# Residual adds of mixer and FFN by accumulating transfers, one rule for the fast rstd, and a planner that knows a shared port

## The chip, the cores and the metric

The kernel runs on one core of one Trainium2 chip. The metric is the time of one execution on the device in microseconds (us), the median of several. The engines of the core run side by side, each in the order of its own queue: TensorE (PE, matmul), VectorE (DVE), ScalarE (ACT), GpSimd (POOL) and SyncE (SP, which here only issues transfers). They wait for each other and for the transfers (DMA) on semaphores.

## The reference

One layer of a streaming encoder, for 1024 prompt frames and 64 further frames of a running stream that share the weights: a token mixer, a SwiGLU FFN and a gated embedding, each added to the residual behind an RMSNorm.

```python
hn = _rmsnorm(h, pre_mix_g)
proj = hn @ w_in
...
mix = jnp.concatenate([y.astype(h.dtype), pool_out.astype(h.dtype)], axis=-1) @ w_out
h = h + _rmsnorm(mix, post_mix_g)
hn = _rmsnorm(h, pre_ffn_g)
f = (jax.nn.silu(hn @ w_gate) * (hn @ w_up)) @ w_down
h = h + _rmsnorm(f, post_ffn_g)
gate = jax.nn.sigmoid((h @ w_ple_gate).astype(f32))
e = (p_i @ w_ple_proj).astype(f32) * gate
h = h + _rmsnorm(e, ple_norm_g).astype(h.dtype)
```

The width is 1024, the FFN's 2816. What is left out above is the mixer's inside: a causal convolution, a chunked state-space scan with a SiLU gate, and pooling over trailing windows. The two lines of `h = h + _rmsnorm(...)` behind mixer and FFN are what the change touches.

## The kernel before

**Tiling.** Features lie on the 128 partitions, in eight pages (1024 features); tokens lie along the free dimension, 1088 of them in four chunks of 272 (0 to 3). Every fp32 operand of a matmul is split into a high and a low part, and a product takes three passes (high x high, low x high, high x low), each a matmul of 128x128 by 128x272. Most of ACT's casts (the high part) and DVE's subtractions `sub` (L400, the low part) make such pairs.

**Stages.** In-projection and convolution, scan and pooling, out-projection; behind it the mixer's end by chunk; then the FFN in two phases, in a Strassen-like form that works on pairs of chunks (`h_T`, `h_B` and their combinations are its inputs); behind it the FFN's end by chunk, and the gated embedding with `w_pg` (PE L493, L476).

**The mixer's end, `post_mix`.** Of a chunk, the squares of the out-projection are summed, and `rstd_job` makes 1/rms of it: PE sums over the partitions with four small matmuls (L511), DVE does nine operations on 68x4 (L516 to L545), and PE spreads the result over the partitions with four transposes (L549). Then `two(i)`, for each of four pairs of pages: x is loaded to a half page `xr` by SP; DVE multiplies the pages of `mixf` by rstd (L1402); POOL adds x (L1408, the letter 'G' in `XM`). When two pairs are added, SP stores them as h1 to DRAM. ACT squares the sum (L601), DVE adds the squares (L608, L619), a second `rstd_job` makes the rstd of h (tile `t_h`), and `norm` (L1433) multiplies by it. From this come `h_T` and `h_B`: cast (L1453), low part (L400), differences (L1465).

**The FFN's end, `post_ffn`.** The same with `f`: scale on ACT (L2057), load of h1 to `hr`, multiply (L2064), add on POOL (L2067, 'G' in `XF`) or on DVE (L2070, 'D'), cast to the high page of h (L2074), low page (L400). PE takes these pages at L493, in their order.

**The start.** `w_in0` comes in two halves, with the four x pages of the first chunk between and behind them, all by SP; ACT casts the weights (L827) and makes x (L731), and PE begins at L914.

**What sets the order.** The kernel's text isn't the order of the queues. The class `Layout` is a planner that runs when the kernel is built: every job is a generator that yields (engine, cost in us, wait), and the planner keeps one clock for each engine and puts the instruction that could start first next. PE's work is the base on which time goes forward (`tick`, cost of a matmul from `mmt`). On the chip, each engine then runs its queue in order, and waits where the estimate was too early. In `rstd_job`, the flag `f` (0 if `fast`, else 1) sets how long the sums and the transposes are held back in the plan after what they need: with `fast` not at all, without it the transposes by 3 pieces of PE's work.

Of the kernel before, what the change touches and what calls it, by code (L numbers as in the profile page):

```python
# [11 lines left out]
ALU = mybir.AluOpType  # L12
# [11 lines left out]
ORD_X = (0, 1, 2, 3)  # L24
# [10 lines left out]
XM, XF, XP = 'GGGG', 'GDGD', 'GDDD'  # L35
# [14 lines left out]
P_XP = 3  # L50
# [7 lines left out]
P_DTC = 4  # L58

# [4 lines left out]
TW = -1  # L64
X_LATE = 18
NK = 8
# [147 lines left out]
class Layout:  # L214
# [7 lines left out]
    def __init__(self):  # L222
        self.now = T0
        self.seq = 0
        self.jobs = []
        self.busy = {"A": BA, "D": BD, "G": 0.0}
        self.done = 0.0
        self.mem = 0.0
        self.rate = RATE
        self.fill = []  # L230
        self.filling = False
# [8 lines left out]
    def step(self, job):  # L240
        self.done = job["t"]
        try:
            req = next(job["gen"])
        except StopIteration:
            return False
        finally:
            self.done = 0.0
        job["req"] = req
        if not callable(req):
            wait = req[2] if len(req) > 2 else 0  # L250
            job["ready"] = max(job["t"] + (HOP if req[0] != job["eng"] else HOPS), wait) if isinstance(wait, At) else job["t"] + (0.04 if wait == TW else wait * self.PIECE if wait >= 3 else HOP if req[0] != job["eng"] else HOPS)
        return True
# [6 lines left out]
    def tick(self, length=None):  # L259
        self.now += (length or self.PIECE / 2)  # L260
        far = self.now + AHEAD
        while True:
# [35 lines left out]
            eng, cost = job["req"][:2]  # L298
            self.busy[eng] = job["t"] = start + cost
# [25 lines left out]
def trunk(ctx, tc, xT, par, wmix, wdt, poolw, wout, wff, wdn, wpg, wpp, pT, ssm0,  # L325
# [58 lines left out]

    cp = const.tile([P, PWIDTH], F32, name="cp")
# [28 lines left out]
    def wjob(name, src, tag, bufs, ready=None, width=2 * NK * P, raw=None, at=None, free=None, start=None, keep=lambda: 0):  # L414
# [3 lines left out]
        def gen():  # L418
# [29 lines left out]
            yield ("D", 1.23)  # L448
# [16 lines left out]
    def mmt(n):  # L465

        return (1.0625 * n + 14) / 2400
# [119 lines left out]
    class SumSq:  # L587
# [8 lines left out]
        def job(self, src, used):  # L596
# [7 lines left out]
            if first:  # L604
                self.acc = sq
            else:
                yield ("D", 0.8)
                ve.tensor_tensor(self.acc, self.acc, sq, ALU.add)  # L608
                n2.give(sq)
# [7 lines left out]
        def whole(self):  # L617
            yield ("D", 0.45)
# [109 lines left out]
    def x_split(c, k, rv, at, used):  # L728
# [3 lines left out]
        yield ("D", 0.51)  # L732
# [5 lines left out]
    def x_square(c, k, rv, at, used):  # L738
# [15 lines left out]
        if k:  # L754
            yield (add_e, 0.45 if add_e == "D" else 0.92)
# [75 lines left out]
    def w0_low(h, hs):  # L831
        yield ("D", 0.6)
# [15 lines left out]
    def x_job():  # L848
        for c in ORD_X[1:]:
            for k2 in range(4):  # L850
# [34 lines left out]
    def conv_post(i):  # L885
# [4 lines left out]
        for w_ in range(1, 4):  # L890
            yield ("D", 1.38)
# [36 lines left out]
    for i in range(4):  # L928
        donew(f"in{i}")
# [125 lines left out]
    def ssd(c):  # L1055
# [32 lines left out]
        yield ("D", 0.7, 0)  # L1088
# [6 lines left out]
        for b in range(4):  # L1095
            yield ("A", 0.24, 0)
# [14 lines left out]
        for g in range(2):  # L1111
            yield ("D", 0.68, 0)
# [6 lines left out]
        else:  # L1119
# [5 lines left out]
            yield ("D", 0.68, 0)  # L1125
# [58 lines left out]
    def pool_post(gi):  # L1184
# [7 lines left out]
        for step in range(gi + 1):  # L1192
# [4 lines left out]
            yield ("D", 1.25, 0)  # L1197
# [7 lines left out]
        yield ("D", 1.25)  # L1205
# [8 lines left out]
        yield ("D", 1.25, 1)  # L1214
        sub(ve, plo[:, HIST:], cur[:, HIST:], ph[:, HIST:])
        exts.give(cur)
        for c, (t0, L) in enumerate(CH):
# [9 lines left out]
            for s, ln, grp, pos in chunk_parts(c):  # L1227
                o = HIST + SEQ - f if grp else t0 - f
                yield ("A", 0.14 + ln * 0.0011, 1)
# [43 lines left out]
    def z_job(i, c, ps, zz):  # L1273
# [10 lines left out]
        for s, n, v in parts_view(i, c):  # L1284
            yield ("D", 0.12 + n * 0.00125, 1)
# [4 lines left out]
    def gate(c, zz):  # L1290
# [3 lines left out]
        for g in range(2):  # L1294
# [7 lines left out]
            yield ("D", 0.45)  # L1302
# [15 lines left out]
    def mix_split(c, i):  # L1318
# [3 lines left out]
        for s, n, v in parts_view(i, c):  # L1322
            yield ("D", 0.12 + n * 0.00125)
# [62 lines left out]
    def post_mix(c, mf, ss):  # L1386
# [7 lines left out]
        def two(i):  # L1394
            yield n2.ok
            xr = n2.take(f"xr{c}_{i}")
            yield ("S", 0, 0)
            at = dma(xr, xT[c][:, 2 * i:2 * i + 2], 2 * L)
# [7 lines left out]
            if XM[i] == "G":  # L1406
                yield ("G", 1.6, at)
                gp.tensor_tensor(v, v, xr, ALU.add)  # L1408
            else:
                yield ("D", 0.73, at)  # L1410
                ve.tensor_tensor(v, v, xr, ALU.add)
            n2.give(xr)
# [17 lines left out]
        def norm(m, r2, left):  # L1430
            v = mf[m // 4][:, m % 4, :]
            yield ("D", 0.45, 0)
# [8 lines left out]
    def hforms(p):  # L1441
# [5 lines left out]
        def form(f, src):  # L1447
# [4 lines left out]
            yield ("A", 0.78, 1)  # L1452
            ac.copy(vs[0], src)  # L1453

            def low():
                yield ("D", 1.06)
# [6 lines left out]
        def add(dst, x, y):  # L1463
            yield ("D", 1.06)
# [66 lines left out]
    def weight_stream(units):  # L1531
        def form(u, f, src):
# [22 lines left out]
            def low():  # L1555
                yield ("D", 0.15 + 0.133 * u.ks)
# [11 lines left out]
        def add(u, dst, x, y, op):  # L1568
            yield ("D", 0.15 + 0.133 * u.ks, 1)
# [60 lines left out]
    def evac(q, m):  # L1630
# [4 lines left out]
        def finish(blk, t):  # L1635
# [7 lines left out]
            else:  # L1643
                yield lambda: blk in q.gate.a
                g = q.gate.a[blk]
                yield ("D", tD)
# [56 lines left out]
    def aforms(q):  # L1703
# [5 lines left out]
        def form(f, t):  # L1709
# [7 lines left out]
            def low():  # L1717
                yield ("D", tD)
# [14 lines left out]
        def add(dst, x, y):  # L1733
            yield ("D", tD)
# [39 lines left out]
    def p_piece(c):  # L1774
# [7 lines left out]
        yield ("D", 0.73)  # L1782
# [7 lines left out]
    def proj_group(c, m):  # L1790
        def emit():
# [5 lines left out]
            def job():  # L1797
                yield nts.ok
                e_ = nt(f"e{c}_{m}")
                yield ("A", 0.48, 1)  # L1800
# [245 lines left out]
    def post_ffn(c, ss, prio):  # L2046
# [6 lines left out]
        def two(i):  # L2053
# [4 lines left out]
            yield n2.ok  # L2058
            hr = n2.take(f"hr{c}_{i}")
            yield ("S", 0, 0)  # L2060
            at = dma(hr, h1_d[c][:, 2 * i:2 * i + 2], 2 * L)
            yield lambda: bool(flag)
            yield ("D", 1.0, 0)
            ve.tensor_tensor(v, v, flag[0][:, :L].unsqueeze(1).broadcast_to([P, 2, L]), ALU.mult)  # L2064
            if XF[i] == "G":
                yield ("G", 1.6, at)
                gp.tensor_tensor(v, v, hr, ALU.add)  # L2067
            else:
                yield ("D", 0.73, at)
                ve.tensor_tensor(v, v, hr, ALU.add)  # L2070
            n2.give(hr)
# [3 lines left out]
            yield ("D", 0.73)  # L2075
# [10 lines left out]
    def post_ple(c, ss, rest):  # L2086
# [7 lines left out]
        def two(i):  # L2094
            e = E[c][i // 2][:, i % 2 * 2:i % 2 * 2 + 2]
            yield ("D", 0.82)
# [8 lines left out]
            elif how[i] == "G":  # L2105
                yield ("G", 1.6)
                gp.tensor_tensor(e, e, fp2(c, i), ALU.add)
            else:
                yield ("D", 0.73)
# [47 lines left out]
    for c in ORD_E:  # L2157
# [7 lines left out]
        for i in range(4):  # L2165
# [8 lines left out]
            def job(i=i, d=d, c=c, e=e, sume=sume, scale=scale):  # L2174
# [6 lines left out]
                yield ("D", 0.73, EL[c, i][1])  # L2181
# [5 lines left out]
            def job6(i=i, d=d, c=c, e=e, sume=sume, scale=scale):  # L2187
# [10 lines left out]
                yield ("D", 0.45)  # L2198
# [144 lines left out]
```

## Time and profile before

| | us |
|---|---|
| median of 3 runs | 1225.96 |
| runs | 1224.27 to 1226.66 |
| profiled execution, its time | 1226.61 |
| profiled execution, its span | 1224.8 |
| PE busy | 1200.6 |
| mean granted clock of PE | 0.993 |

A busy row of PE is a stretch in which matmuls follow one another; its idle time and the granted clock are where time can be lost. In the lists of waits, "A <- B" is an instruction of A that stood until B was done. A row of the timeline gives its start, its length, engine, line, operation and tiles, how many equal ones follow (x), and, in brackets, how long the engine stood just before and for what. In a window's row, each engine has its busy time and, in brackets, its instructions; then the granted clock, the DMA engines' mean busy share and GB/s.

### The profile page before, as it was taken

The page shows a single profiled execution, that of the slowest core. Times are in us where ns is not written, and L with a number is a line of the kernel's source. Part 1 is how long each engine was busy: PE and PEld are TensorE (multiplying, and loading weights), DVE is VectorE, ACT ScalarE, POOL GpSimd, SP SyncE. Part 2 cuts the span into 40 slices and gives each one's busy share as a digit, 9 for nine tenths or more (in the row PEclk, how much of TensorE's full clock was granted, in tenths as well). Part 3 has the DMA queues.
Part 4 walks back from the last instruction along what each step waited for, and adds up shares of the span by engine and source line. Part 5 has one row for each costly group of instructions (what it writes and reads, how often), then busy time and mean ns, then how long its engine had stood idle before and what let it go on. Part 6 is the DMA issues. An engine that isn't in the chain of part 4 may idle for free.

```text
span 1224.8 us, 23784 instructions
## 1 busy us (share of the span) xinstructions
PE 1200.6 (98%) x9641; PEld 1180.8 (96%) x9641; DVE 872.8 (71%) x1572; ACT 571.8 (47%) x1119; POOL 69.4 (6%) x56
## 2 busy tenths in 40 slices
PE   8999999999999999999999999999999999999997
PEld 6999999999999899999999999999999999999996
DVE  5697787874898776676677576766646655688875
ACT  6365557854456444443444444444432212356543
POOL 2000000120232000000000000000000000001111
PEclk8999999999999999999999999999999999999998
DMA  6122133243354144443443344336978676334422
GB/s 224 45 74 88 54 110 106 61 124 119 123 175 161 64 133 153 161 151 119 143 162 135 125 153 162 116 140 244 394 299 287 217 254 220 127 108 128 138 82 83
DMA packets 73777, 182.56 MB, mean 149 GB/s; under 512 B 8700, under 2 KB 17220, under 8 KB 73668
## 3 DMA queue, kind: packets, MB, share of 16 engines
q1 hardware_dynamic: 73668, 181.06, 42.9%
q8 instruction: 75, 1.23, 0.4%
q14 instruction: 34, 0.28, 0.1%
HBM read 122.03 MB, written 59.00 MB: 148 GB/s over the span
## 4 chain that ended last, share of the span: by engine, by line
PE 62%; DVE 3%; DMA 2%; POOL 0%; ACT 0%; issue 0%; DVEq 0%; ACTq 0%; POOLq 0%; SPq 0%
PE psall L1618 54%; PE psall L476 6%; PE psall L493 2%; DMA al_B<-af_dram 1%; POOL mixf L1408 0%; DMA raw_d<-in_wdn_dram 0%; DVE f L1881 0%; PE psall L511 0%; DMA raw_pg<-in_wpg_dram 0%; DVE mixf L1433 0%; DVE sq_f L608 0%; PE psall L549 0%; DMA e_dram<-e 0%; DVE mixf L1402 0%; DVE mixf L1465 0%
## 5 line engine op out<-in xcount | busy, mean ns | idle before, releaser
L476 PE MATMUL psall<-x,w_in 128*128 128x272 f32 x1440 | 193.8, 291 | 0.0
L476 PEld LDWEIGHTS psall<-x,w_in 128*128 128x128 f32 x1440 | 184.0, 188 | 3.3 <-issue 2.8
L1881 DVE TENSOR_TENSOR f<-f,psall 128x544 f32<-128x544 f32 (+1 forms) x96 | 60.7, 638 | 69.3 <-PE psall L1618 67.7
L1618 PE MATMUL psall<-h_T,w_g_S 128*128 128x272 f32 x792 | 102.9, 290 | 2.2 <-DVE h_T L400 1.8
L1618 PEld LDWEIGHTS psall<-h_T,w_g_S 128*128 128x128 f32 x792 | 101.1, 191 | 2.6 <-DVE h_T L400 2.0
L1618 PE MATMUL psall<-al_T,w_d_S 128*128 128x272 f32 x768 | 100.1, 289 | 1.0 <-ACT sq_f L601 0.5
L1618 PE MATMUL psall<-h_T,w_u_S 128*128 128x272 f32 x792 | 100.7, 287 | 0.0
L1618 PEld LDWEIGHTS psall<-h_T,w_u_S 128*128 128x128 f32 x792 | 99.6, 188 | 0.0
L1618 PEld LDWEIGHTS psall<-al_T,w_d_S 128*128 128x128 f32 x768 | 97.6, 188 | 1.7 <-ACT sq_f L601 0.7
L476 PE MATMUL psall<-mix,w_out 128*128 128x272 f32 x720 | 93.3, 289 | 0.0
L476 PEld LDWEIGHTS psall<-mix,w_out 128*128 128x128 f32 x720 | 90.9, 188 | 0.0
L1618 PE MATMUL psall<-al_B,w_d_A 128*128 128x272 f32 x528 | 72.1, 289 | 2.6 <-DVE w_d_A L400 2.6
L476 PE MATMUL psall<-h,w_pg 128*128 128x272 f32 x576 | 74.3, 289 | 0.0
L476 PEld LDWEIGHTS psall<-h,w_pg 128*128 128x128 f32 x576 | 72.7, 188 | 0.0
L1618 PEld LDWEIGHTS psall<-al_B,w_d_A 128*128 128x128 f32 x528 | 68.4, 188 | 3.1 <-DVE w_d_A L400 3.1
L1618 PE MATMUL psall<-h_B,w_g_A 128*128 128x272 f32 x528 | 70.2, 288 | 0.1
L1618 PE MATMUL psall<-h_B,w_u_A 128*128 128x272 f32 x528 | 69.7, 288 | 0.0
L1618 PEld LDWEIGHTS psall<-h_B,w_g_A 128*128 128x128 f32 x528 | 67.7, 188 | 0.3 <-ACT e L1801 0.3
L1618 PEld LDWEIGHTS psall<-h_B,w_u_A 128*128 128x128 f32 x528 | 67.5, 188 | 0.0
L1546 ACT CAST w_d_A<-raw_d 128x512 fp32r<-128x512 f32 (+3 forms) x44 | 22.3, 523 | 69.9 <-PE psall L1618 35.1
L1546 ACT CAST w_d_S<-raw_d 128x512 fp32r<-128x512 f32 (+3 forms) x54 | 26.5, 532 | 57.7 <-DVE raw_d L1570 33.9
L2067 POOL TENSOR_TENSOR f<-f,sq_f 128x544 f32<-128x544 f32 x5 | 7.4, 1479 | 726.8 <-DVE f L2064 721.3
(401 smaller groups left out, 2246.0 us busy)
## 6 DMA issues: line engine op xcount, KB each, us to landing
af_dram<-a_T SPq DMA_DIRECT2D x88, 272.0 KB, 2.3
al_T<-af_dram SPq DMA_DIRECT2D x44, 544.0 KB, 5.6
af_dram<-a_B SPq DMA_DIRECT2D x66, 272.0 KB, 2.2
al_B<-af_dram SPq DMA_DIRECT2D x33, 544.0 KB, 5.9
raw_g<-in_wff_dram SPq DMA_DIRECT2D x22, 512.0 KB, 4.1
raw_u<-in_wff_dram SPq DMA_DIRECT2D x22, 512.0 KB, 3.7
raw_in<-in_wmix_dram SPq DMA_DIRECT2D x15, 512.0 KB, 3.8
raw_d<-in_wdn_dram SPq DMA_DIRECT2D x14, 512.0 KB, 5.3
```

What stands on the lines that cost most here:

```text
L476: pe.matmul(out, lhsT, rhs, start=i == 0, stop=i == n - 1)
L493: pe.matmul(out, w.v(wi, k), act.v(xi, k, L), start=first and n == 0, stop=not left and n == 2)
L1546: ac.copy(v[:, 0], src)
L1618: pe.matmul(d[:, p - q.ps[0], :], w.v(wi, k), u.b(bf, xi, p, k), start=start and not k and not wi and not xi, stop=k == u.ks - 1 and wi == ...
L1881: ve.tensor_tensor(v[:, sl], v[:, sl], src[:, pl], ALU.add)
L2067: gp.tensor_tensor(v, v, hr, ALU.add)
```

## The change

Four things are changed.

1. In mixer and FFN, `XM` and `XF` are all 'A'. There is then no load of x or h1 to a half page, and no add on POOL or DVE: behind the multiply, POOL issues a transfer (`dma_add`) that brings the two pages and adds them to `mixf` or `f` in place. That is 16 transfers for the mixer and 16 for the FFN, in place of as many loads from SP's queue, of 24 adds on POOL and of 8 on DVE. The next user (the square, the cast, the store of h1) waits for the transfer.
2. `FAST_M` and `FAST_H` give the fast rule of `rstd_job` to m and h of all chunks.
3. The planner gets the kind "E": a DVE operation with two inputs in SBUF, which it never lets run at the same time as a POOL operation (`port`). Some 25 costs are changed, among them a matmul's (14 to 12 in `mmt`).
4. At the start, the second x page goes ahead of the second half of `w_in0`, the small `wdt` behind all x pages, and the first two x pages of the next chunk ahead of further weights. The in-projection's weights of a group are freed chunk by chunk in the last round.

```diff
-XM, XF, XP = 'GGGG', 'GDGD', 'GDDD'
+XM, XF, XP = 'AAAA', 'AAAA', 'GDDD'
...
+FAST_M, FAST_H = (0,1,2,3), (0,1,2,3)
...
-                if callable(req) or req[0] not in self.busy:
+                if callable(req) or req[0] not in "ADEG":
                     continue
-                start = max(job["ready"], self.busy[req[0]])
+                start = max(job["ready"], self.busy["D" if req[0] == "E" else req[0]])
+                if req[0] in "EG":
+                    start = max(start, self.port["G" if req[0] == "E" else "E"])
...
+            if eng in "EG":
+                self.port[eng] = start + cost
+            if eng == "E":
+                eng = "D"
...
+    def dma_add(dst, src, cols):
+
+        gp.dma_start(dst, src, accum_op=ALU.add)
+        return lay.load(cols)
...
-        return (1.0625 * n + 14) / 2400
+        return (1.0625 * n + 12) / 2400
...
-        xr0 += [x_dma(C0, k2) for k2 in ((0,), (1, 2, 3))[h]]
-        if not h:
-            dt_at = dma(wdr, wdt, NK * 8)
+        xr0 += [x_dma(C0, k2) for k2 in ((0, 1), (2, 3))[h]]
+    dt_at = dma(wdr, wdt, NK * 8)
...
-    dma(cp[:, PFIRST:], par[:, PFIRST:], PWIDTH - PFIRST)
+    xr1 = [x_dma(ORD_X[1], k2) for k2 in range(2)]
     for i in (2, 3):
+        if i == 3:
+            dma(cp[:, PFIRST:], par[:, PFIRST:], PWIDTH - PFIRST)
...
-            yield ("D", 1.0, 0)
+            yield ("D", 0.72, 0)
             ve.tensor_tensor(v, v, flag[0][:, :L].unsqueeze(1).broadcast_to([P, 2, L]), ALU.mult)
...
-            if XM[i] == "G":
-                yield ("G", 1.6, at)
+            if XM[i] == "A":
+                yield ("S", 0, 0)
+                yield ("S", 0, dma_add(v, xT[c][:, 2 * i:2 * i + 2], 2 * L))
+            elif XM[i] == "G":
+                yield ("G", 1.35, at)
                 gp.tensor_tensor(v, v, xr, ALU.add)
...
-        yield from rstd_job(ss.halves(), L, 1024.0, f"m{c}", flag, free=ss.free)
+        yield from rstd_job(ss.halves(), L, 1024.0, f"m{c}", flag, fast=c in FAST_M, free=ss.free)
...
-            yield from rstd_job(ss2.halves(), L, 1024.0, f"h{c}", got, free=ss2.free)
+            yield from rstd_job(ss2.halves(), L, 1024.0, f"h{c}", got, fast=c in FAST_H, free=ss2.free)
...
-            if XF[i] == "G":
-                yield ("G", 1.6, at)
+            if XF[i] == "A":
+                yield ("S", 0, 0)
+                yield ("S", 0, dma_add(v, h1_d[c][:, 2 * i:2 * i + 2], 2 * L))
+            elif XF[i] == "G":
+                yield ("G", 1.35, at)
                 gp.tensor_tensor(v, v, hr, ALU.add)
```

The lines move by 10 to 30 in the changed kernel: L511 becomes L527, L549 L565, L476 L492, L493 L509, L400 L416, L2064 L2089, L1618 L1642, L1881 L1905.

How the order moves is shown at three places. On PE, the h sums of the first chunk (four small matmuls on `cp` and a sum of squares, here `sq_m`), before:

```order
L476 MATMUL psall<-mix_10_3010,w_out_3176 128x272 x4
L476 MATMUL psall<-mix_11_3011,w_out_3176 128x272 x4
L476 MATMUL psall<-mix_00_3008,w_out_3177 128x272 x4
L476 MATMUL psall<-mix_01_3009,w_out_3177 128x272 x4
L511 MATMUL psall<-cp,sq_m_3542 68x1 [waits DVE_49]
L511 MATMUL psall<-cp,sq_m_3542 68x1 x3
L476 MATMUL psall<-mix_00_3008,w_out_3257 128x272 [waits Activation_49]
L476 MATMUL psall<-mix_00_3008,w_out_3257 128x272 x3
```

and changed:

```order
L492 MATMUL psall<-mix_01_2944,w_out_3071 128x272 x4
L492 MATMUL psall<-mix_10_2945,w_out_3071 128x272 x4
L492 MATMUL psall<-mix_11_2946,w_out_3071 128x272 [waits Pool_49] x4
L492 MATMUL psall<-mix_00_2943,w_out_3072 128x272 x2
L527 MATMUL psall<-cp,sq_m_3536 68x1 [waits DVE_49]
L527 MATMUL psall<-cp,sq_m_3536 68x1 x3
L492 MATMUL psall<-mix_00_2943,w_out_3072 128x272 x2
L492 MATMUL psall<-mix_01_2944,w_out_3072 128x272 x4
```

Between the transposes of the chunk's first rstd (`t_m`) and these sums stood 123 matmuls of 128x272; now there are 66.

Also on PE, the transposes of the last chunk's h rstd (`t_h`) among the FFN's first matmuls, before:

```order
L1618 MATMUL psall<-h_T_0_4324,w_g_S_4136 128x272
L1618 MATMUL psall<-h_T_1_4325,w_g_S_4136 128x272
L1618 MATMUL psall<-h_T_0_4324,w_g_S_4136 128x272 x2
L1618 MATMUL psall<-h_T_1_4325,w_g_S_4136 128x272
L1618 MATMUL psall<-h_T_0_4324,w_g_S_4136 128x272
L549 MATMUL psall<-cp,t_h_4801 128x68 [waits DVE_49]
L549 MATMUL psall<-cp,t_h_4801 128x68 x3
L1618 MATMUL psall<-h_T_0_4324,w_g_S_4136 128x272
```

and changed:

```order
L1642 MATMUL psall<-h_B_1_4115,w_g_A_3704 128x272
L1642 MATMUL psall<-h_B_0_4114,w_g_A_3704 128x272
L1642 MATMUL psall<-h_T_0_4317,w_g_S_4116 128x272 [waits Activation_49]
L1642 MATMUL psall<-h_T_1_4318,w_g_S_4116 128x272
L1642 MATMUL psall<-h_T_0_4317,w_g_S_4116 128x272
L565 MATMUL psall<-cp,t_h_4790 128x68 [waits DVE_49]
L565 MATMUL psall<-cp,t_h_4790 128x68 x3
L1642 MATMUL psall<-h_T_0_4317,w_g_S_4116 128x272
```

Between the sums and these transposes stood 39 matmuls, and now 18; the sums themselves stand 7 matmuls further back among the FFN's matmuls.

On DVE, the FFN's end of the first chunk, before from its second multiply on, and changed from the first subtraction that makes `h` to the last (the tiles `f_0` are this chunk's, `f_1` those of the next, still being summed), before:

```order
L2064 TENSOR_TENSOR f_0_9784<-f_0_9784,psall 128x2x272
L1881 TENSOR_TENSOR f_1_9918<-f_1_9918,psall 128x272 [waits PE_49]
L1881 TENSOR_TENSOR f_1_9918<-f_1_9918,psall 128x272 [waits DVE_49,PE_49]
L400 TENSOR_TENSOR h_0_10_12328<-f_0_10202,h_0_00_12326 128x544 [waits Activation_49]
L1881 TENSOR_TENSOR f_0_9917<-f_0_9917,psall 128x272 [waits PE_49]
L2070 TENSOR_TENSOR f_0_9784<-f_0_9784,sq_f_12309 128x2x272 [waits DMAHW5_49]
L1881 TENSOR_TENSOR f_1_9918<-f_1_9918,psall 128x272 [waits PE_49]
L2064 TENSOR_TENSOR f_0_9917<-f_0_9917,psall 128x2x272
L400 TENSOR_TENSOR h_0_10_12328<-f_0_9784,h_0_00_12326 128x544 [waits Activation_49]
L2064 TENSOR_TENSOR f_0_10026<-f_0_10026,psall 128x2x272
L2070 TENSOR_TENSOR f_0_10026<-f_0_10026,hr_3_12383 128x2x272 [waits DMAHW2_49,DVE_49]
L608 TENSOR_TENSOR sq_f_12021<-sq_f_12021,sq_f_12309 128x544
```

and changed:

```order
L1905 TENSOR_TENSOR f_1_9895<-f_1_9895,psall 128x272 [waits DVE_49,PE_49]
L416 TENSOR_TENSOR h_0_10_12305<-f_0_10179,h_0_00_12303 128x544 [waits DMASW0_49,Activation_49]
L1905 TENSOR_TENSOR f_0_9894<-f_0_9894,psall 128x272 [waits PE_49]
L416 TENSOR_TENSOR h_0_10_12305<-f_0_9761,h_0_00_12303 128x544 [waits DMASW1_49,Activation_49]
L1905 TENSOR_TENSOR f_1_9895<-f_1_9895,psall 128x272 [waits PE_49]
L2089 TENSOR_TENSOR f_0_10008<-f_0_10008,psall 128x2x272
L416 TENSOR_TENSOR h_0_11_12306<-f_0_9894,h_0_01_12304 128x544 [waits DMASW2_49,Activation_49]
L624 TENSOR_TENSOR sq_f_11998<-sq_f_11998,sq_f_12286 128x544
L635 TENSOR_TENSOR sq_f_11998<-sq_f_11998 128x272 [waits DVE_49]
L416 TENSOR_TENSOR w_pg_12332<-raw_pg_12167,w_pg_12331 128x1024 [waits DMAHW1_49]
L416 TENSOR_TENSOR w_pg_12342<-raw_pg_12223,w_pg_12341 128x1024 [waits DMAHW2_49]
L416 TENSOR_TENSOR h_0_11_12306<-f_0_10008,h_0_01_12304 128x544 [waits DMASW3_49,Activation_49]
```

The subtractions that make `h` now wait for a transfer (DMASW), the fourth multiply stands behind the second of them, and two subtractions of weights stand ahead of the last one.

More of the change, by code (lines that the diff above doesn't have):

```diff
@@ L226, in __init__ @@
         self.busy = {"A": BA, "D": BD, "G": 0.0}
+        self.port = {"E": 0.0, "G": 0.0}
         self.done = 0.0
@@ L250, in step @@
             wait = req[2] if len(req) > 2 else 0
-            job["ready"] = max(job["t"] + (HOP if req[0] != job["eng"] else HOPS), wait) if isinstance(wait, At) else job["t"] + (0.04 if wait == TW else wait * self.PIECE if wait >= 3 else HOP if req[0] != job["eng"] else HOPS)
+            eng = "D" if req[0] == "E" else req[0]
+            job["ready"] = max(job["t"] + (HOP if eng != job["eng"] else HOPS), wait) if isinstance(wait, At) else job["t"] + (0.04 if wait == TW else wait * self.PIECE if wait >= 3 else HOP if eng != job["eng"] else HOPS)
         return True
@@ L848, in x_job @@
     def x_job():
+        for k2 in range(2):
+            x_spawn(ORD_X[1], k2, *xr1[k2], P_XP)
         for c in ORD_X[1:]:
-            for k2 in range(4):
+            for k2 in range(2 if c == ORD_X[1] else 0, 4):
                 yield xsem.ok
@@ L927, in trunk @@
             conv_group(i, c, getw(f"in{i}"), i == 0)
-    for i in range(4):
-        donew(f"in{i}")
+            if c == ORD_X[-1]:
+                donew(f"in{i}")
     NH = 8 * NSSD
@@ L1394, in two @@
         def two(i):
[L1395 to L1398, printed above, removed]
+            if XM[i] != "A":
+                yield n2.ok
+                xr = n2.take(f"xr{c}_{i}")
+                yield ("S", 0, 0)
+                at = dma(xr, xT[c][:, 2 * i:2 * i + 2], 2 * L)
             yield lambda: bool(flag)
             v = mf[i // 2][:, i % 2 * 2:i % 2 * 2 + 2, :]
-            yield ("D", 1.0, 0)
+            yield ("D", 0.72, 0)
             ve.tensor_tensor(v, v, flag[0][:, :L].unsqueeze(1).broadcast_to([P, 2, L]), ALU.mult)
```

92 lines of the change are left out of this document (48 added, 44 removed).

## Prediction

> **What bounds the kernel now.** I read the page's first part, then busy time by windows, then TensorE's list of waits, and last the rows around the longest waits. All times are us unless marked.
>
> ```profile
> span 1224.8 us, 23784 instructions
> PE 1200.6 (98%) x9641; PEld 1180.8 (96%) x9641; DVE 872.8 (71%) x1572; ACT 571.8 (47%) x1119; POOL 69.4 (6%) x56
> ```
>
> TensorE (PE) is busy 1200.6 of 1224.8, and the change leaves its matmuls as they are. So all that can be won is the 24 in which PE stands, and what a slower clock takes after a stand. POOL, which loses most of its work here, is at 6%: its own time is worth nothing, only the moments at which its results arrive. The windows tell where PE stands:
>
> ```profile
> core 0: us, PE busy (x) PEld busy (x) DVE busy (x) ACT busy (x) POOL busy (x), PEclk, DMA share, GB/s
> 0.00:25.00 25.00, 21.52 (x128) 17.31 (x129) 13.78 (x33) 14.80 (x31) 8.69 (x11) 0.86 0.75 264
> 375.00:400.00 25.00, 22.64 (x181) 21.74 (x181) 21.85 (x43) 15.22 (x35) 7.43 (x4) 1.00 0.48 174
> 400.00:425.00 25.00, 22.68 (x170) 21.96 (x169) 18.73 (x34) 12.04 (x22) 0.00 (x0) 0.93 0.15 51
> 875.00:900.00 25.00, 22.38 (x176) 21.93 (x175) 17.30 (x33) 11.78 (x25) 0.00 (x0) 1.00 1.02 402
> 1100.00:1125.00 25.00, 22.50 (x181) 21.42 (x180) 21.42 (x48) 16.34 (x29) 2.98 (x2) 1.00 0.39 114
> 1175.00:1200.00 25.00, 25.00 (x207) 25.00 (x206) 17.37 (x32) 9.99 (x18) 2.35 (x3) 1.00 0.16 56
> ```
>
> Three of these stages hold what is edited: the start, the mixer's end (375 to 425) and the FFN's end (1100 to 1125). The last row gives the unit: a full window takes 207 matmuls, 0.121 each. At 875 the DMA engines are full (402 GB/s); nothing there is edited. The waits by name:
>
> ```profile
> engine line waited for: us in total, times, longest us
> PE psall L914 <- ACT x L731: 2.1, 2, 1.8
> PE psall L1618 <- DVE h_T L400: 1.8, 1, 1.8
> PE psall L1618 <- DVE f L1881: 1.5, 3, 0.5
> PE psall L493 <- DVE h L400: 1.2, 2, 0.8
> ```
>
> Two stands of 1.8 cost more than themselves, since the granted clock falls behind them. First the one at the mixer's end, then the one at the start:
>
> ```profile
> 416.00:418.00 2.00, 0.39 (x1) 1.00 0.00 0
> 418.00:420.00 2.00, 1.54 (x7) 0.53 0.00 0
> 420.00:422.00 2.00, 2.00 (x12) 0.62 0.00 0
> 8.00:10.00 2.00, 1.05 (x3) 0.63 0.99 380
> 10.00:12.00 2.00, 1.92 (x19) 0.50 1.05 425
> ```
>
> Busy time times the missing clock from 418 to 422 is 1.54 x 0.47 + 2.00 x 0.38 = 1.5: the 1.83 stand for h_T costs 3.3 in all.
>
> **The change, part by part. First the price of an accumulating transfer.** The trace of before has none. Its nearest rows are the loads that the transfers replace:
>
> ```profile
> sq_m<-in_x_dram SPq DMA_DIRECT2D x9, 272.0 KB, 3.4
> hr<-h_dram SPq DMA_DIRECT2D x8, 272.0 KB, 2.8
> p<-in_x_dram SPq DMA_DIRECT2D x2, 272.0 KB, 5.1
> ```
>
> A plain load of this size takes 2.8 (from h1) or 3.4 (from x); the slowest takes 5.1. An add must also fetch its destination: 278,528 bytes at the 402 GB/s above are 0.7. I take D = 3.5 in the FFN and 4.1 in the mixer, by the rows nearest to each. The ends of the range are 2.8 (the second fetch hidden) and 5.1; below 2.8 there is no reason to go, as at least the same bytes move.
>
> A rule of the Trainium skill bears on this, on both sides. "DMA: Bandwidth & Descriptors", section "Anatomy of one DMA — SWDGE (gpsimd) path", fits transfers issued by GpSimd with 2.0 us plus bytes over 436e3: 2.6 here, an estimate, below the rows, and silent on the add; the sum below would be about -5.5. Its section "Specifications" gives such a transfer a first byte about 0.4 later than one issued by SyncE, which speaks against the change: with that on top, the sum would be about -1. No run here has yet shown a transfer from that queue.
>
> **Mixer's end, last chunk.** Around its two rstd computations before stand:
>
> ```profile
> 388.70 0.40 PE L549 MATMUL psall<-cp,t_m 68*128 68x68 f32 x4
> 389.14 2.62 DVE L1402 TENSOR_TENSOR mixf<-mixf,psall 128x544 f32<-128x544 f32 x4 [1.54 <-PE psall L549]
> 395.02 2.41 POOL L1408 TENSOR_TENSOR mixf<-mixf,xr 128x544 f32<-128x544 f32 x1
> 397.46 0.66 ACT L601 ACTIVATE sq_m<-mixf 128x544 f32<-128x544 f32 x1 [1.14 <-POOL mixf L1408]
> 399.36 0.72 DVE L608 TENSOR_TENSOR p<-p,sq_m 128x544 f32<-128x544 f32 x1
> 400.60 0.43 DVE L619 TENSOR_TENSOR p<-p 128x272 f32<-128x272 f32 x1
> 401.54 0.60 PE L511 MATMUL psall<-cp,p 128*68 128x1 f32 x8
> 403.80 0.16 DVE L545 SCALAR_TENSOR_TENSOR t_h<-t_h 68x4 f32<-68x4 f32 x1
> 406.98 0.40 PE L549 MATMUL psall<-cp,t_h 68*128 68x68 f32 x4
> 407.49 1.72 DVE L1433 SCALAR_TENSOR_TENSOR mixf<-mixf,cp,psall 128x272 f32<-128x272 f32 x4 [2.06 <-PE psall L549]
> 418.45 2.86 PE L1618 MATMUL psall<-h_T,w_g_S 128*128 128x272 f32 x11 [1.83 <-DVE h_T L400]
> ```
>
> rstd of h is ready at 403.96, but its transposes are queued on PE only at 406.98; DVE stood 2.06 for them and then works without a pause until the h_T that PE misses at 416.6. In the changed order the transposes come 18 matmuls after their sums, not 39, and the sums 7 later: 14 x 0.121 = 1.7 earlier. Of the stand of 1.83 a tenth is left, and with it the clock stays up: **-3.2**. This holds if the sums are not late. From the m transposes to the sums takes: the four multiplies end 391.76, 3.1 after; D; then one square, one add, one fold (0.66 + 0.72 + 0.43, with the hops 2.0). Together 5.1 + D = 9.2. The new order has 81 matmuls there, 9.8: covered. If the cover goes (D over 4.7), each us beyond is lost again.
>
> **Mixer, first chunk.** The same distance was 123 matmuls and is 66 now, 8.0, because the rule for a fast rstd is applied to all chunks. 9.2 - 8.0 makes PE stand: **+1.2**. Behind the waiting squares on ACT stand those of the next chunk's PSUM; PE needs them only at sums that are behind this stand in its own queue, so they add nothing. The chunks between have 10 or more: nothing.
>
> **FFN's end, first chunk** (1100 to 1115):
>
> ```profile
> 1103.55 0.71 DVE L2064 TENSOR_TENSOR f<-f,psall 128x544 f32<-128x544 f32 x1
> 1104.24 0.44 DVE L1881 TENSOR_TENSOR f<-f,psall 128x272 f32<-128x272 f32 x1
> 1104.34 1.36 POOL L2067 TENSOR_TENSOR f<-f,sq_f 128x544 f32<-128x544 f32 x1 [706.92 <-DVE f L2064]
> 1105.73 0.65 ACT L2074 CAST h<-f 128x544 fp32r<-128x544 f32 x1 [1.41 <-POOL f L2067]
> 1106.89 0.72 DVE L400 TENSOR_TENSOR h<-f,h 128x544 fp32r<-128x544 f32 x1
> 1113.90 2.26 PE L493 MATMUL psall<-h,w_pg 128*128 128x272 f32 x16 [0.79 <-DVE h L400]
> ```
>
> Here the add was quick (1.36 on POOL), and D takes its place. The first page's multiply starts at about the same time: its sums stand 12 matmuls before the transposes instead of 21, but nine times 0.16 of rstd lie between in both. It ends 1104.26; one L1881 and the second multiply (0.44 + 0.71) end 1105.4. Its transfer lands 1108.9, cast and subtraction (0.65 + 0.72) end 1110.3. Only behind that subtraction stands the fourth multiply: 1111.0, its transfer 1114.5, cast and subtraction 1115.9, and 12 matmuls on it: 1117.3. Before, the last wait ended at 1113.90 with 23 matmuls to go: 1116.7. That is **+0.6**, and D enters twice: each us of D costs 2 here. At D = 2.8 it is -0.8, at 5.1 +3.8. The changed DVE queue now also holds evacuations of PSUM (L1881 before) behind subtractions that wait for a transfer (until 1108.4, against 1106.89); I add the longest such wait of PE before, **+0.5**.
>
> **Start.** The second x page goes ahead of the second half of the first weights (256 KB, 0.65 at 402 GB/s) and of a small one: the stand of 1.8 for x becomes about 1.1, -0.7. A us less at a clock of 0.5 is worth 0.5. I take **-1.2**; the bounds are 0 (the second half of the weights is now late by as much) and -3 (all of the stand and the clock behind it).
>
> **The rest at nothing:** the remaining chunks' loads go from SP's queue (32 of them) and as many transfers come; DVE loses eight adds where it isn't the bound; in the other windows PE is full, which hides both. The planner's new costs and its port rule reorder DVE and POOL there; what they do, within a us either way, I can't read from rows. The order of the last 12 us is nearly the same.
>
> **Sum:** -3.2 + 1.2 + 0.6 + 0.5 - 1.2 = -2.1. It is made against the profiled execution, 1226.61 (span 1224.8 and 1.81 around it), which is 0.65 above the median of the runs, 1225.96. So 1224.5 for such an execution, and **1223.9** for the median.
>
> **The rivals.**
>
> *The transfers land late (slower).* Mechanism: an accumulating transfer, issued by POOL, takes 5.1 like the slowest load, 5.7 in the mixer. The FFN's end pays 3.8 + 0.5, and its stands, now over 1.8, the 1.5 of clock. The first chunk pays 5.1 + 5.7 - 8.0 = 2.8. The last chunk's sums are 1.0 late, so the transposes gain 0.7 rather than 1.7, and of the 3.2 only 0.7 is left. With -1.2 that is +6.7: 1232.7. In D the sum grows threefold (once in the first chunk, twice in the FFN), so it turns slower from D = 4.2 in the FFN, 4.8 in the mixer. For it: the 5.1 row, the second fetch, four transfers at once. Against: most loads take 3.6 or less, and the DMA share where they run is 0.48 and 0.39.
>
> *Like a plain load (faster still).* D = 2.8 and 3.4: first chunk +0.5, FFN -0.8, no late evacuation: -4.7, 1221.3. By the Trainium skill's fit above it would be this case. For it: the engines have bandwidth to spare there.
>
> *The gain doesn't come (same).* DVE has other work in the queue ahead of the missing h_T, so the 1.7 is filled and PE stands as before, while the costs come: +1.1, 1227.1. Against it: DVE's 2.06 of idle just ahead of the chain.
>
> *The change doesn't do what it says for the time.* 24 adds leave POOL and 8 leave DVE, but neither sets the end in most chunks; then all terms are small and it is about 1226.
>
> **How the numbers follow.** A measurement of this kernel tells about 0.2%, 2.5, from no change. Chances: forecast 0.38, plain load 0.23, late 0.21, gain doesn't come 0.13, no effect 0.05. The forecast lies next to the edge of 1223.5: 0.18 of it counts as faster, 0.18 as same, 0.02 as slower. Faster: 0.18 + 0.23 + 0.01 = 0.42. Slower: 0.02 + 0.21 + 0.03 = 0.26. Same: 0.32. The range goes up to the late case, 1233, and down to the plain load with the start's full gain and 2.5 more from waits that the planner's new costs might shift: 1217. Near the likeliest alone it is 1222 to 1226.
>
> **What would show it.** The transfers' row: 3 to 4.2 from issue to landing. PE's wait for h_T near 418 gone and the clock 1.00 from 418 to 422. A stand of about 1 before the first chunk's h sums. The stretch of w_pg at 1108 to 1117 not shorter. The second wait for x in the start near 1. It is wrong if a transfer takes over 4.5, if the granted clock falls at a place where it held before, or if the planner's new order makes a stand in a stage that I put at nothing.

## The result, and the profile after

The changed kernel takes **1296.59 us** in the median of 4 runs (1294.12 to 1298.99); the kernel before, beside it, 1225.14. The ratio is 1.0582 (95% interval 1.057 to 1.0595): 71 us slower. The forecast was 1223.9, its range ended at 1233. The profiled execution has a span of 1293.8.

The page's first part and, from its list of transfers, the two new rows (KB each, median us from issue to landing), with the packets of the software queue, which the kernel before doesn't have:

```profile
span 1293.8 us, 23732 instructions
PE 1221.9 (94%) x9641; PEld 1199.2 (93%) x9641; DVE 850.0 (66%) x1564; ACT 577.8 (45%) x1123; POOL 62.8 (5%) x64
...
q0 software_dynamic: 6656, 8.91, 4.9%
...
mixf<-in_x_dram POOLq DMA_DIRECT2D x16, 272.0 KB, 6.0
...
f<-h_dram POOLq DMA_DIRECT2D x16, 272.0 KB, 4.7
```

PE has the same 9641 matmuls, but stands 72 us instead of 24. A transfer takes 6.0 and 4.7, where the prediction took 4.1 and 3.5. The same four stages as windows, before and then after (busy time of each engine, granted clock, DMA share, GB/s):

```profile
0.00:300.00 300.00, 295.82 (x2406) 282.21 (x2407) 221.65 (x470) 177.65 (x410) 23.47 (x27) 0.99 0.30 99
300.00:450.00 150.00, 144.15 (x1163) 141.99 (x1163) 124.06 (x227) 78.48 (x149) 27.42 (x16) 0.99 0.39 132
450.00:1075.00 625.00, 622.38 (x4965) 621.59 (x4964) 411.40 (x641) 240.86 (x421) 0.00 (x0) 1.00 0.53 187
1075.00:1225.00 150.00, 138.26 (x1114) 135.00 (x1112) 115.67 (x236) 74.87 (x140) 18.55 (x13) 0.97 0.34 108
```

```profile
0.00:300.00 300.00, 296.08 (x2410) 282.16 (x2411) 220.19 (x470) 183.04 (x414) 22.45 (x27) 0.99 0.30 95
300.00:450.00 150.00, 134.56 (x1043) 132.80 (x1042) 103.52 (x210) 73.11 (x138) 14.25 (x16) 0.94 0.46 123
450.00:1095.00 645.00, 643.47 (x5126) 642.64 (x5126) 427.84 (x670) 248.94 (x437) 0.00 (x0) 1.00 0.54 185
1095.00:1294.00 199.00, 147.80 (x1069) 141.56 (x1067) 98.42 (x216) 72.68 (x135) 26.07 (x21) 0.85 0.35 80
```

Up to 300 both have done the same (2406 and 2410 matmuls). At 450 the changed kernel is 116 matmuls behind, some 14 us at 0.12 each. The FFN itself runs at full rate in both. The last stage has 51 us in which PE stands, and a mean granted clock of 0.85. So the loss lies in the stages where the transfers are. PE's waits by name (us in total, times, longest):

```profile
PE psall L527 <- DVE el L635: 20.6, 2, 14.9
PE psall L527 <- DVE sq_f L635: 12.7, 1, 12.7
PE psall L492 <- ACT e L1825: 6.6, 3, 3.7
PE psall L509 <- ACT h L2103: 5.5, 4, 2.6
PE psall L527 <- DVE sq_m L635: 4.5, 1, 4.5
PE psall L527 <- ACT mixf L1518: 3.3, 1, 3.3
...
PE psall L1642 <- DVE h_T L416: 0.2, 1, 0.2
```

The last row is the wait that was to go: 1.8 before, 0.2 now. The first two rows, 33 us, are sums for an rstd, and what they wait for is not a transfer. It is work on DVE and ACT that has its inputs, but stands in their queues behind casts and subtractions of h that wait for one. The stand of 12.7 shows it: the last add into the tile is done at 1167.2, and its fold (L635) runs only at 1179.72, behind two such subtractions and what is queued with them. The two stands of the first row end likewise, behind such a cast on ACT. Here are DVE's rows ahead of the stand of 12.7 (not all of them) and PE's:

```profile
1166.51 0.72 DVE L624 TENSOR_TENSOR sq_f<-sq_f,el 128x544 f32<-128x544 f32 x1
...
1170.92 0.72 DVE L416 TENSOR_TENSOR h<-f,h 128x544 fp32r<-128x544 f32 x1 [3.06 <-ACT h L2103]
1175.92 0.72 DVE L416 TENSOR_TENSOR h<-f,h 128x544 fp32r<-128x544 f32 x1 [4.27 <-ACT h L2103]
...
1179.72 0.43 DVE L635 TENSOR_TENSOR sq_f<-sq_f 128x272 f32<-128x272 f32 x1
1180.21 1.07 PE L527 MATMUL psall<-cp,sq_f 128*68 128x1 f32 x8 [12.67 <-DVE sq_f L635]
```

POOL's timeline shows why the transfers come so late. First the mixer's first chunk, then the FFN's (start, length, how many, what POOL stood for just before):

```profile
312.96 2.81 POOL L398 DMA_DIRECT2D mixf<-in_x_dram  x3 [32.24 <-DVE mixf L1422]
317.43 0.89 POOL L398 DMA_DIRECT2D mixf<-in_x_dram  x1 [1.65 <-issue]
...
1118.61 1.20 POOL L398 DMA_DIRECT2D f<-h_dram  x1 [707.37 <-DVE f L1905]
1124.59 1.22 POOL L398 DMA_DIRECT2D f<-h_dram  x1 [4.78 <-PE psall L1642]
1129.93 1.20 POOL L398 DMA_DIRECT2D f<-h_dram  x1 [4.13 <-issue]
1134.91 1.22 POOL L398 DMA_DIRECT2D f<-h_dram  x1 [3.79 <-issue]
```

In the mixer three transfers are issued back to back, and the fourth only 4.5 after the first, about when the first has landed (the shortest of all took 4.2). In the FFN each waits for the one ahead of it: some 5 us each, 20 a chunk, four chunks. DVE, which runs in order, stands behind it for the casts:

```profile
1125.28 0.73 DVE L416 TENSOR_TENSOR h<-f,h 128x544 fp32r<-128x544 f32 x1 [2.70 <-ACT h L2103]
1125.92 0.43 DVE L1905 TENSOR_TENSOR f<-f,psall 128x272 f32<-128x272 f32 x1
1130.29 0.72 DVE L416 TENSOR_TENSOR h<-f,h 128x544 fp32r<-128x544 f32 x1 [3.93 <-ACT h L2103]
1130.93 0.43 DVE L1905 TENSOR_TENSOR f<-f,psall 128x272 f32<-128x272 f32 x1
1131.28 0.71 DVE L2089 TENSOR_TENSOR f<-f,psall 128x544 f32<-128x544 f32 x1
1135.33 0.73 DVE L416 TENSOR_TENSOR h<-f,h 128x544 fp32r<-128x544 f32 x1 [3.34 <-ACT h L2103]
```

The fourth multiply (L2089) is done only at 1132.0, as it is queued behind the second waiting subtraction (1130.29). Here that costs nothing by itself: its transfer is issued 2.9 later still, at 1134.91, when the third has landed.

### The profile page after: what moved, and what is told of

It reads as the page before. It is cut to its first block, busy times and chain, and to the rows that moved or that the text cites. A ratio compares the mean times of both kernels' runs of the same rounds, so it can differ in the third digit from the quotient of the medians.

```text
span 1293.8 us, 23732 instructions
## 1 busy us (share of the span) xinstructions
PE 1221.9 (94%) x9641; PEld 1199.2 (93%) x9641; DVE 850.0 (66%) x1564; ACT 577.8 (45%) x1123; POOL 62.8 (5%) x64
## 3 DMA queue, kind: packets, MB, share of 16 engines
q0 software_dynamic: 6656, 8.91, 4.9%
## 5 line engine op out<-in xcount | busy, mean ns | idle before, releaser
L492 PE MATMUL psall<-x,w_in 128*128 128x272 f32 x1440 | 193.7, 291 | 0.0
L492 PEld LDWEIGHTS psall<-x,w_in 128*128 128x128 f32 x1440 | 184.0, 188 | 3.3 <-issue 2.8
L1905 DVE TENSOR_TENSOR f<-f,psall 128x544 f32<-128x544 f32 (+1 forms) x96 | 60.3, 636 | 66.1 <-PE psall L1642 65.4
L1642 PE MATMUL psall<-h_T,w_g_S 128*128 128x272 f32 x792 | 102.0, 288 | 0.2 <-DVE h_T L416 0.2
L1642 PE MATMUL psall<-al_T,w_d_S 128*128 128x272 f32 x768 | 100.5, 289 | 1.0 <-ACT sq_f L617 0.4
L1642 PE MATMUL psall<-h_T,w_u_S 128*128 128x272 f32 x792 | 101.2, 288 | 0.0
L1642 PEld LDWEIGHTS psall<-h_T,w_g_S 128*128 128x128 f32 x792 | 100.3, 188 | 0.5 <-DVE h_T L416 0.4
L1642 PEld LDWEIGHTS psall<-h_T,w_u_S 128*128 128x128 f32 x792 | 100.0, 188 | 0.0
L1642 PEld LDWEIGHTS psall<-al_T,w_d_S 128*128 128x128 f32 x768 | 97.7, 188 | 1.9 <-ACT sq_f L617 0.6
L492 PE MATMUL psall<-mix,w_out 128*128 128x272 f32 x720 | 97.6, 297 | 0.0
L492 PEld LDWEIGHTS psall<-mix,w_out 128*128 128x128 f32 x720 | 95.0, 196 | 0.0
L492 PE MATMUL psall<-h,w_pg 128*128 128x272 f32 x576 | 77.6, 296 | 0.0
L492 PEld LDWEIGHTS psall<-h,w_pg 128*128 128x128 f32 x576 | 76.0, 196 | 0.1
L1642 PE MATMUL psall<-al_B,w_d_A 128*128 128x272 f32 x528 | 71.8, 288 | 1.5 <-DVE w_d_A L416 1.4
L1642 PEld LDWEIGHTS psall<-al_B,w_d_A 128*128 128x128 f32 x528 | 68.3, 188 | 1.9 <-DVE w_d_A L416 1.7
L1642 PE MATMUL psall<-h_B,w_g_A 128*128 128x272 f32 x528 | 70.0, 288 | 0.0
L1642 PE MATMUL psall<-h_B,w_u_A 128*128 128x272 f32 x528 | 69.6, 287 | 0.0
L1642 PEld LDWEIGHTS psall<-h_B,w_g_A 128*128 128x128 f32 x528 | 67.6, 188 | 0.0
L1642 PEld LDWEIGHTS psall<-h_B,w_u_A 128*128 128x128 f32 x528 | 67.5, 188 | 0.0
L398 POOL DMA_DIRECT2D f<-h_dram x16 | 19.3, 1209 | 785.3 <-DVE f L1905 707.4
L416 DVE TENSOR_TENSOR w_u_S<-raw_u,w_u_S 128x512 fp32r<-128x512 f32 x44 | 30.3, 688 | 27.1 <-ACT w_u_S L1570 26.6
```

Of the source, the lines that this page charges most:

```text
L398: gp.dma_start(dst, src, accum_op=ALU.add)
L416: eng.tensor_tensor(lo, src, hi.bitcast(F32), ALU.subtract)
L492: pe.matmul(out, lhsT, rhs, start=i == 0, stop=i == n - 1)
L1642: pe.matmul(d[:, p - q.ps[0], :], w.v(wi, k), u.b(bf, xi, p, k), start=start and not k and not wi and not xi, stop=k == u.ks - 1 and wi == ...
L1905: ve.tensor_tensor(v[:, sl], v[:, sl], src[:, pl], ALU.add)
```

## Experiments

Ratios are to runs of the kernel before taken beside each experiment, with their 95% intervals. Differences in us are of medians where nothing else is said.

### One part undone

**e_none**: the letters back, all else as changed.

```diff
-XM, XF, XP = 'AAAA', 'AAAA', 'GDDD'
+XM, XF, XP = 'GGGG', 'GDGD', 'GDDD'
```

> XM and XF back to the letters of before (GGGG, GDGD), all else as changed: planner's costs and port, fast rstd, start. Theory 1 (the accumulating transfers are the whole loss): 1219 to 1227, PE's waits for sq_f and el at L527 (33 us in all) gone. Rival (the planner's new rule or the fast rstd lose time by themselves): 1235 or more.

1233.48, ratio 1.0067 (1.0052 to 1.0082), between the two theories: 63 of the 71 us go, but 7.5 stay without any accumulating transfer, with a wait on PE in the FFN's first matmuls that the kernel before doesn't have:

```profile
409.09 4.71 PE L1642 MATMUL psall<-h_T,w_g_S 128*128 128x272 f32 x22 [5.95 <-DVE w_g_S L416]
```

**e_xf** and **e_xm**: only one of the two letters back.

```diff
-XM, XF, XP = 'AAAA', 'AAAA', 'GDDD'
+XM, XF, XP = 'AAAA', 'GDGD', 'GDDD'
```

> Only the FFN's adds back on POOL and DVE (XF GDGD); the mixer keeps its transfers. Theory 1, with the losses as read by stage (mixer's end about 16 us of stands and clock, FFN's end about 50): 1237 to 1246. Rival (the mixer's transfers are hidden and the loss there is the planner's): about 1225.

1243.19, ratio 1.015 (1.0135 to 1.0165), within the first theory's range.

```diff
-XM, XF, XP = 'AAAA', 'AAAA', 'GDDD'
+XM, XF, XP = 'GGGG', 'AAAA', 'GDDD'
```

> Only the mixer's adds back on POOL (XM GGGG); the FFN keeps its transfers. Theory 1: 1270 to 1284. Rival (a late mixer delays the FFN's end, most of the loss begins there): below 1250.

1286.77, ratio 1.0498 (1.0481 to 1.0516), 2.8 above the first theory's range and far from the rival's. Against e_none, the mixer's transfers (e_xf) cost 9.7 and the FFN's (e_xm) 53.3; with the 7.5 that makes 70.5 of the 71. The FFN's loss does not begin in the mixer. The sum fits, though each letter makes another plan (the wait for w_g_S above isn't in the changed kernel's list), so the 7.5 and the 9.7 are not sure one by one.

### How many transfers are in flight

**e_lay**: as changed, but the tile f is laid out so that a transfer's destination is one run on each partition.

```diff
-F[q.i, th] = slots.take(f"f{q.i}_{th}", F32, True).rearrange("p (h c t) -> p h c t", h=2, c=2)
+F[q.i, th] = slots.take(f"f{q.i}_{th}", F32, True).rearrange("p (c h t) -> p h c t", h=2, c=2)
```

> As changed, but the FFN's tile f is laid out chunk before page, so that a transfer's destination is one run of 2176 bytes on each partition instead of two of 1088: 144 packets each instead of 272; queues and semaphores are the same instruction by instruction. Theory A (the software queue takes no new transfer when its packets in flight would pass some 500: three transfers of 144 in the mixer, one of 272 in the FFN): up to three FFN transfers are issued back to back, a chunk's four land in about 10 us instead of 20, time 1250 to 1272. Theory B (accumulating transfers into f go one at a time whatever their shape): one in flight, 1293 to 1299.

1261.96, ratio 1.0296 (1.0278 to 1.0313): 35 us gone by the shape of a tile. Its page's queue row and POOL in the second chunk's FFN end:

```profile
q0 software_dynamic: 4608, 8.91, 4.5%
...
1145.72 2.79 POOL L398 DMA_DIRECT2D f<-h_dram  x3 [18.91 <-DVE f L2089]
1151.32 0.88 POOL L398 DMA_DIRECT2D f<-h_dram  x1 [2.81 <-issue]
```

4608 packets for 32 transfers are 144 each. In the changed kernel it was 6656: 16 x 144 for the mixer leave 4352, 272 for each of the FFN's. With the same bytes and the same 23732 instructions, up to three are now in flight and the fourth waits, as in the mixer. On the other engines the new layout changes no time (the multiply of f takes 0.71, the cast 0.65, the subtraction 0.72 in both kernels), so no other effect of it accounts for the 35. Theory B falls.

**b_gpload**: the kernel before, its loads of x issued by POOL, without accumulation.

```diff
-            at = dma(xr, xT[c][:, 2 * i:2 * i + 2], 2 * L)
+            gp.dma_start(xr, xT[c][:, 2 * i:2 * i + 2])
+            at = lay.load(2 * L)
```

> The kernel before, with the mixer's 16 loads of x issued by POOL as plain transfers to the half pages (no accumulation); the adds stay on POOL. If the limit of three in flight belongs to the queue: the fourth of a chunk is issued only when the first has landed, also here. If it belongs to the accumulation: four back to back. If accumulating is what makes a transfer of 272 KB take 4.2 to 8 us: 3 to 4 here; if the queue: also 4 to 6.

1225.63, ratio 1.0004 (0.9993 to 1.0014).

```profile
q0 software_dynamic: 1280, 4.46, 1.1%
...
306.61 0.69 POOL L1398 DMA_DIRECT2D sq_m<-in_x_dram  x1 [29.23 <-DVE sq_m L608]
307.29 1.07 POOL L1398 DMA_DIRECT2D xr<-in_x_dram  x2
308.35 0.54 POOL L1398 DMA_DIRECT2D sq_m<-in_x_dram  x1
...
xr<-in_x_dram POOLq DMA_DIRECT2D x5, 272.0 KB, 4.2
```

Four back to back: plain, a transfer is 80 packets (1280 / 16), so four are 320. All the cases fit a limit of packets in flight on this queue: 320 and 3 x 144 = 432 go, 2 x 272 = 544 and 4 x 144 = 576 don't. Where between 432 and 544 it lies, and whether it counts packets or something that goes with them, wasn't tried. The plain transfer takes 0.54 of POOL's time to issue, against 0.89 with accumulation in 128 runs and 1.2 in 256. From issue to landing it takes 4.2 to `xr` and 4.3 to `sq_m`; from SP's queue, in the kernel before, the same rows had 3.6 and 3.4. So 0.6 to 0.9 come with the queue. The other 1.7 to 1.8 of the mixer's 6.0 come with accumulating in 144 packets beside two others in flight, and the runs don't part these: f's took 4.7 alone in flight, with 272 packets, and 5.6 in e_lay, with 144 and up to three in flight. The Trainium skill ("DMA: Bandwidth & Descriptors", "Anatomy of one DMA — SWDGE (gpsimd) path") gives 2.6 for this size by its fit, an estimate; the 4.2 decides here. Its later first byte for this queue, by about 0.4 ("Specifications"), has the sign of the 0.6 to 0.9.

### The plan around the transfers

**e_lay_late**: e_lay, and the planner counts 3 us more for such a transfer.

```diff
-        return lay.load(cols)
+        return At(lay.load(cols) + 3)
```

> The kernel with f laid out chunk before page (1262.0), and the planner told that an accumulating transfer takes 3 us longer (some 6, not 3). If what is left of the loss is that DVE and ACT are queued with other work behind waits for a transfer: the plan puts that work first, 1240 to 1254. Rival (what is left is the chain of transfer and low page that PE has no other work for): 1257 to 1266.

1244.84, ratio 1.015 (1.0132 to 1.0169): as the first theory has it, 17 us of what was left go when the plan knows the longer wait and puts other work ahead of it.

**b_acc**: the changed kernel without the planner's edits, that is before with fast rstd, start and all transfers.

```diff
...
-            if XF[i] == "G":
-                yield ("G", 1.6, at)
-                gp.tensor_tensor(v, v, hr, ALU.add)
...
+            yield ("S", 0, 0)
+            yield ("S", 0, dma_add(v, h1_d[c][:, 2 * i:2 * i + 2], 2 * L))
...
```

> The changed kernel without the planner's edits: fast rstd, start and all 32 accumulating transfers, on the costs and the rule of before. If the transfers cost the same whatever the plan (70 us on a base of 1218): 1278 to 1292, with one FFN transfer in flight. Rival (the new costs are what made the plan blind to the transfers, and the old ones hide more): below 1270.

1279.32, ratio 1.0435 (1.0415 to 1.0455). The transfers lose 62 on the old plan too (its base, 1217.2, is b_best, below), and 63 on the new one (e_none), so they are the main loss whatever the plan. The planner's edits (costs, port rule and early release together) add 17 here. Without the transfers they add as much: e_none is 16 above b_best, from which it differs by these edits alone. So the two losses simply add up.

**b_acc_mend**: b_acc with both remedies, f's layout and the 3 us.

> All 32 transfers on the planner of before, with both faults mended: f laid out chunk before page, and 3 us more in the plan for a transfer. If serial issue and the plan's blindness are the whole price of the transfers: 1217 to 1223, level with the same kernel without them (1217.2). Rival (a transfer's latency stays on the path where PE has nothing else to do): 1227 to 1240.

1224.23, ratio 0.9995 (0.9985 to 1.0004), between the two ranges. Of the 62, 55 are gone: they were serial issue and a plan that didn't know the latency. Some 7 (8 by the ratios) stay against b_best. Part of it is as the rival says, since PE still stands for h at L500 and for e at L483, where b_best has 0.2 or less for each; the rest was not placed:

```profile
PE psall L500 <- ACT h L2066: 2.6, 2, 1.8
PE psall L483 <- ACT e L1802: 2.2, 2, 1.9
```

### The other parts, each alone on the kernel before

**b_fast**: the fast rstd alone.

```diff
...
-        yield from rstd_job(ss.halves(), L, 1024.0, f"m{c}", flag, free=ss.free)
+        yield from rstd_job(ss.halves(), L, 1024.0, f"m{c}", flag, fast=c in FAST_M, free=ss.free)
...
```

> The kernel before with the fast rule of rstd for m and h of all chunks alone. If the rule is what took 1.8 us at the h transposes of the last chunk with the old adds: 1225 to 1230, with a wait for t_h. Rival (the transposes come earlier and the wait for h_T goes, as forecast): 1222 to 1224.

1219.48, ratio 0.9956 (0.9941 to 0.997): faster, by more than either theory. Its windows of the mixer's end (before: 22.64 and 22.68, clock 0.93 in the second) and PE's rows there:

```profile
375.00:400.00 25.00, 24.85 (x208) 1.00 0.61 218
400.00:425.00 25.00, 23.80 (x186) 1.00 0.00 1
```

```profile
396.42 0.60 PE L513 MATMUL psall<-cp,sq_m 128*68 128x1 f32 x8
399.22 0.40 PE L551 MATMUL psall<-cp,t_h 68*128 68x68 f32 x4
```

The transposes of h follow the sums after 2.8, where it was 5.4; no wait for h_T is left, and the clock stays at 1.00. PE's waits for e in this stage, 2.3 in all in the kernel before, are down to 0.2 as well.

**b_start**: the order of the first loads alone.

```diff
-        xr0 += [x_dma(C0, k2) for k2 in ((0,), (1, 2, 3))[h]]
-        if not h:
-            dt_at = dma(wdr, wdt, NK * 8)
+        xr0 += [x_dma(C0, k2) for k2 in ((0, 1), (2, 3))[h]]
+    dt_at = dma(wdr, wdt, NK * 8)
...
```

> The kernel before with the start's edits alone (order of the first loads and the next chunk's first two x pages early). If the start is worth what the changed kernel's first window says (136 matmuls by 25 us, not 128: about 1 us): 1224 to 1225. Rival (the work is done sooner and waits later, or the planner reorders the rest and loses): 1226 or more.

1224.13, ratio 0.9989 (0.998 to 0.9998): 1.4 gained by the ratio, as the first theory has it.

**b_plan**: the planner's edits alone.

```diff
...
-FAST_M, FAST_H = (0,1,2,3), (0,1,2,3)
+FAST_M, FAST_H = (), ()
...
```

(and the letters and the start of before)

> The planner's edits alone (costs, the port rule, early release of the in-projection's weights), with the letters, the rstd rule and the start of before. If the planner's edits are what made the kernel without the transfers slower (1233.5): 1230 to 1236, with the wait of PE for w_g_S near 405. Rival (fast rstd or start did it): 1224 to 1228.

1233.47, ratio 1.0073 (1.0057 to 1.0089). The size is as expected, but PE waits for h_T, not for w_g_S, and the granted clock of that window is 0.81:

```profile
419.09 0.59 PE L1639 MATMUL psall<-h_T,w_g_S 128*128 128x272 f32 x1 [7.19 <-ACT h_T L1474]
```

```profile
400.00:425.00 25.00, 15.80 (x116) 0.81 0.06 21
```

Which of the some 25 costs, the port rule or the early release makes this order wasn't tried one by one. With fast rstd and start added, the new plan takes the same time (e_none, 1233.48): on it these two parts gain nothing.

**b_best**: before with fast rstd and start.

> The kernel before with the two parts that gained by themselves: the fast rstd (1219.5) and the start's order (1224.1). If they add, as their places are apart: 1217 to 1219. Rival (the planner makes another order of both together, and gives one of them back): 1220 to 1224.

1217.16, ratio 0.993 (0.9917 to 0.9942): the parts add, and it beats both kernels. With it the whole difference can be put together from medians: -8.7 for fast rstd and start on the old plan, +16.3 for the planner's edits on top of them, +63.1 for the transfers, 70.7 of the 71.

```profile
PE 1195.7 (98%) x9641; PEld 1177.6 (97%) x9641; DVE 870.4 (72%) x1572; ACT 571.1 (47%) x1119; POOL 65.0 (5%) x56
```

## Why the prediction was wrong, by its steps

- **The step that failed: the FFN's end was priced on the first chunk alone, with each transfer landing D after its own multiply** ("D enters twice: each us of D costs 2 here", +0.6 + 0.5). A chunk's four transfers go one after another, because two of them, 272 packets each, pass what the queue takes (by the limit that all the runs fit). D enters four times a chunk, and in all four chunks, where it becomes the bound of the stage: 53.3 (e_xm against e_none) for 1.1. The multiplies of 128x2x272 in the changed order, two runs on each partition, were in front of me and I read nothing in them; e_lay shows that they were worth 35. The forecast also followed only the chain from multiply to low page. The longest stands, 33 us, are rstd sums whose inputs stand, on DVE and ACT, in the queue behind work that waits for the late pages; of what e_lay left, 17 go with a plan that knows the latency (e_lay_late).
- **"The chunks between have 10 or more: nothing" and "they add nothing"** failed with it in the mixer. The first chunk's stand was rightly placed (4.5 at L527 for sq_m, forecast 1.2), but D was 6.0, not 4.1, and the fourth transfer was held back: its square begins at 322.73, where the forecast's terms have the page landed at 318.7 (3.1 and 4.1 after the transposes at 311.46). What ACT had queued behind the waiting squares was waited for too, in the chunks behind (L1518 3.3; e 6.6, where it was 2.3). The mixer's part measured +9.7, forecast +1.2.
- **"The rest at nothing ... within a us either way"** failed: the planner's edits lose 7.6 on the kernel before, and 16 to 17 on top of fast rstd and start, with the transfers or without. I had said that I couldn't read them from rows; that should have widened the range, not closed it at zero.
- **The last chunk's h_T** was right in mechanism on the old plan: in b_fast the transposes come earlier, the wait and the fall of the clock go. The size was -5.4 for the fast rstd in all (ratio 0.9956), against -3.2 for this one place, where the waits for e that go as well weren't counted; the transfers had no part in it. The 1.5 for the clock in the -3.2 is not a fixed price of such a stand: b_start has the same stand without it (last section). On the new plan the gain doesn't show in the time.
- **The start** was right by itself: -1.4 against -1.2.
- **The late rival** had the direction and the wrong mechanism: with 5.1 for each transfer and the four at once it came to 1232.7. Its D was nearly that of the FFN (4.7). What it lacked is that the queue lets one go at a time in the FFN, so that the price is a rate, not a latency.

## What to carry to other kernels

Before moving many transfers to another queue, ask how many of them that queue holds at once, and count the runs of their destination on each partition: the price of a queue that holds one is the latency times their number. A wait that a planner or an author thinks short costs most where other work stands behind it in an in-order queue, so the estimated latency belongs in the plan before the change is judged. And a change of several parts is worth taking apart even when it loses: here two of its parts were worth 0.7% by themselves, which stayed hidden in e_none, since a third part loses 16 us on top of them.

## What the runs showed of the hardware

- POOL's software queue took up to 432 packets of accumulating transfers in flight (three of 144) and held back the next one where that would have made 544 (two of 272) or 576 (four of 144); POOL stands meanwhile, at the issue.
- A 272 KB transfer was 80 packets plain, 144 accumulating into one run of 2176 bytes on each partition, and 272 into two runs; the issue took 0.54, 0.89 and 1.2 us of POOL.
- A stand of 1.8 of PE for h_T was followed by a granted clock of 0.53 to 0.62 for some 4 us in the kernel before, but not in b_start, where the same window has 1.00 with the same wait (each is one execution):

```profile
PE psall L1621 <- DVE h_T L400: 1.8, 1, 1.8
```

```profile
400.00:425.00 25.00, 22.78 (x182) 1.00 0.10 34
```
